# Split GELU-multiply on one core: stores issued from ScalarE's DMA queue, loads from SyncE's

## The chip, the cores and the metric

One core of one Trainium2 chip; the other cores are idle. The metric is the device time of one execution in microseconds.

## The reference

```python
# x: (32, 512, 2048) float32, standard normal
x1, x2 = x[..., :1024], x[..., 1024:]
out = (0.5 * x1 * (1 + erf(x1 / sqrt(2)))) * x2      # (32, 512, 1024) float32
```

The input is 134.2 MB and the output 67.1 MB. There is one GELU and one multiplication per output element, and no matmul.

## The kernel before

The rows are cut into 16 tiles. Each of the 128 partitions holds R = 8 consecutive rows of a tile, so a load is 8.4 MB (64 KB per partition) and a store is 4.2 MB (32 KB per partition). Both kinds of tile have two buffers. All transfers are issued from SyncE, so they stand in one queue in program order: load 0, load 1, store 0, load 2, store 1, load 3, and so on.

```python
    ahead = [load(0), load(1)]                     # load: nc.sync.dma_start(out=x_tile, in_=x_t[i])
    for i in range(n_tiles):
        x_tile = ahead.pop(0)
        o_tile = opool.tile([P, R, half], out.dtype, name="o_tile")
        pieces = 1 if i < n_tiles - 1 else 4       # the last tile is stored in four pieces
        step = R // pieces
        for k in range(pieces):
            for r in range(k * step, (k + 1) * step):
                nc.scalar.activation(out=x_tile[:, r, :half], in_=x_tile[:, r, :half], func=GELU)
                nc.vector.tensor_mul(out=o_tile[:, r, :], in0=x_tile[:, r, :half], in1=x_tile[:, r, half:])
            rows = slice(k * step, (k + 1) * step)
            nc.sync.dma_start(out=o_t[i][:, rows, :], in_=o_tile[:, rows, :])
        if i + 2 < n_tiles:
            ahead.append(load(i + 2))
```

## Time and profile before

| | before |
|---|---|
| time, median (4 runs) | 475.56 us |
| span of the profile | 472.7 us |
| DVE / ACT busy | 31% / 26% |
| DMA engines busy | 99% |
| tile 1's landing to tile 2's | 29.2 us |
| last load's landing to the end | 20.4 us |

The page of the kernel before: its row of DMA busy tenths in 40 equal slices, and the share of the 16 DMA engines' time that each queue took. Queue q1 is SyncE's; q14 is the runtime's instruction fetch.

```profile
DMA  8999999999999999999999999999999999999996
...
q1 hardware_dynamic: 5040, 201.33, 99.0%
q14 instruction: 2, 0.02, 0.0%
...
out_dram<-o_tile SPq DMA_DIRECT2D x15, 4096.0 KB, 28.5
out_dram<-o_tile SPq DMA_DIRECT2D x4, 1024.0 KB, 8.9
x_tile<-in_x_dram SPq DMA_DIRECT2D x16, 47.6
```

In the last three lines, the last column is the median time from issue to landing. A load lands 47.6 us after its issue, although its bytes need only 19.3 us at 434 GB/s. The rest is standing in the line, because the previous load and a store are ahead of it.

The table of windows of the kernel before. Its columns are the stretch and its length in us, busy time and instruction counts of three engines, the clock, the mean DMA busy share, and GB/s. The borders are the moments when a load had landed.

```profile
22.60:43.06 20.46, 9.17 (x8) 7.68 (x9) 0.00 (x0) 1.00 0.94 384
43.06:72.27 29.21, 9.17 (x8) 7.68 (x8) 0.00 (x0) 1.00 1.00 431
...
423.30:452.30 29.00, 9.17 (x8) 7.68 (x8) 0.00 (x0) 1.00 1.00 434
452.30:472.70 20.40, 9.17 (x8) 7.68 (x8) 0.00 (x0) 1.00 0.80 341
```

In the middle, the DMA share is 1.00 and compute takes a third of each period: the DMA engines bound the kernel. The last stretch has a lower share.

### The profile page before, as it was taken

To read this page: it belongs to the slowest core of one execution; us is meant where nothing else is said; L and a number is where in the kernel's file an instruction comes from. 1 tells how busy PE (TensorE), PEld (TensorE's weight loads), DVE (VectorE), ACT (ScalarE), POOL (GpSimd) and SP (SyncE) were. 2 spreads that over 40 slices of the span, in tenths; PEclk is the share of its full clock that TensorE was granted. 3 is DMA by queue.
4 is the path that set the end of the run, shared out by engine and by line. 5 is a ranking of instruction groups with operands and counts; after the bars stand their busy time and mean duration, and the time that the engine had idled before them with its cause. 6 is when DMAs were issued, how large, how long until landed. Compare 5 with 4: busy or idle time off the path is not lost.

```text
span 472.7 us, 394 instructions
## 1 busy us (share of the span) xinstructions
DVE 146.8 (31%) x128; ACT 124.2 (26%) x129; POOL 0.2 (0%) x4
## 2 busy tenths in 40 slices
DVE  0072507034070340704307043070420705206061
ACT  1053206042060410605106051050501506014060
POOL 0000000000000000000000000000000000000000
DMA  8999999999999999999999999999999999999996
GB/s 355 444 444 380 441 422 444 444 413 474 391 458 427 408 446 427 451 438 402 458 410 460 416 410 455 422 460 433 427 438 397 441 444 433 449 402 469 410 408 291
DMA packets 5042, 201.35 MB, mean 426 GB/s; under 512 B 560, under 2 KB 560, under 8 KB 560
## 3 DMA queue, kind: packets, MB, share of 16 engines
q1 hardware_dynamic: 5040, 201.33, 99.0%
q14 instruction: 2, 0.02, 0.0%
HBM read 134.22 MB, written 67.11 MB: 426 GB/s over the span
## 4 chain that ended last, share of the span: by engine, by line
DMA 79%; DVE 15%; ACT 2%; SPq 1%; issue 0%; DVEq 0%; ACTq 0%
DMA x_tile<-in_x_dram 79%; DVE o_tile L52 15%; ACT x_tile L49 2%; SPq L58 1%; DVEq L86 0%; SPq L37 0%; ACTq L49 0%
## 5 line engine op out<-in xcount | busy, mean ns | idle before, releaser
L52 DVE TENSOR_TENSOR o_tile<-x_tile 128x1024 f32<-128x1024 f32 x128 | 146.8, 1219 | 315.8 <-ACT x_tile L49 315.8
L49 ACT ACTIVATE x_tile<-x_tile 128x1024 f32<-128x1024 f32 x128 | 122.9, 1042 | 335.1 <-DMA x_tile<-in_x_dram 335.1
L49 ACT ACT_TABLE_LOAD x1 | 1.3, 1283 | 0.7 <-PEq L75 0.7
L75 POOL MEMSET const-bfloat16-1.0<- 128x1 bf16 x1 | 0.1, 102 | 0.0
L75 POOL MEMSET const-uint8-127<- 128x1 uint8 x1 | 0.1, 102 | 0.0
L75 POOL MEMSET const-float32-1.0<- 128x1 f32 x1 | 0.1, 99 | 0.0
L75 POOL MEMSET const-float32-0.0<- 128x1 f32 x1 | 0.1, 98 | 0.2 <-issue 0.2
## 6 DMA issues: line engine op xcount, KB each, us to landing
out_dram<-o_tile SPq DMA_DIRECT2D x15, 4096.0 KB, 28.5
out_dram<-o_tile SPq DMA_DIRECT2D x4, 1024.0 KB, 8.9
x_tile<-in_x_dram SPq DMA_DIRECT2D x16, 47.6
```

The lines of the kernel that those rows point to most:

```text
L49: nc.scalar.activation(out=x_tile[:, r, :half], in_=x_tile[:, r, :half], func=GELU)
L52: nc.vector.tensor_mul(out=o_tile[:, r, :], in0=x_tile[:, r, :half], in1=x_tile[:, r, half:],)
L58: nc.sync.dma_start(out=o_t[i][:, rows, :], in_=o_tile[:, rows, :])
L75: nc = _bacc.Bacc("TRN2", target_bir_lowering=False, num_devices=1)
```

## The change

Stores get a queue of their own, ScalarE's, so that loads no longer stand behind a store that waits for compute. The four stores of the last tile go out on SyncE, which has no loads left to issue by then, and so do not stand behind store 14.

```diff
-        pieces = 1 if i < n_tiles - 1 else 4
+        last = i == n_tiles - 1
+        pieces = 4 if last else 1
 ...
-            nc.sync.dma_start(out=o_t[i][:, rows, :], in_=o_tile[:, rows, :])
+            queue = nc.sync if last else nc.scalar
+            queue.dma_start(out=o_t[i][:, rows, :], in_=o_tile[:, rows, :])
```

## The prediction

> What bounds the kernel now. The DMA engines. The page gives queue q1 a 99.0% share of the 16 engines' span; DVE is 31% busy, ACT 26%. The table of windows gives one tile's period, 43.06 to 72.27 us, as 29.2 us at a DMA share of 1.00 and 431 GB/s; 423.3 to 452.3 us ran at 434 GB/s. All 201.33 MB at 434 GB/s need 464 us (estimate); the span is 472.7 us. The 9 us between lie at the two ends: the start of the first load, and the last stretch, 452.3 to 472.7 us, at a share of 0.80 and 341 GB/s.
>
> The chain of waits is 79% "DMA x_tile<-in_x_dram", 15% DVE. That looks like load latency (47.6 us from issue to landing, against 19.3 us of transfer at 434 GB/s), but most of it is standing in a full line: at its issue, most of the previous load and one store are ahead of it. Taking the store out of that line does not shorten the total line.
>
> What changes. Nothing is added or removed in bytes, transfers or compute. Fifteen 4 MB stores get issued from ACT; four 1 MB stores remain on SyncE. SyncE saves 15 issues of about 0.34 us; ACT pays about as much, 5 us in all. ACT waits 335 us for loads, and at a tile's end the next load is still some 19 us away, so this costs nothing. Load i+2 is issued about 0.45 us earlier, into a line with some 19 us of work in it: worth nothing.
>
> What moves is the order on the DMA engines. Now load i+1 passes wholly before store i. After, the two rings are served in turn: the Trainium skill ("DMA: Bandwidth & Descriptors", section "Issuing engines are not separate DMA queues") says that transfers of several issuers run on the same 16 engines and interleave, and that only issue time is saved. No run shows it yet. I expect the period to stay at 29.2 us, and store i done long before its buffer is wanted again, two tiles later.
>
> The tail. Now the last load lands at 452.3 us with about 4 MB of store 14 still to go, which covers the 10.2 us of the last tile's compute. After, store 14 shares with load 15, so the last load lands later, perhaps at 456 to 460 us, with less store work left to cover the compute; then 10.2 us of compute, about 2.4 us for the last 1 MB and 1 to 2 us to its landing. That gives 471.5 to 474.5 us of span, against 472.7. The unprofiled time stood 2.9 us above the profiled span; so about 476 us.
>
> Predicted: 476.0 us, 8 in 10 between 471.5 and 482. Faster by over 2%: 0.02 (that needs under 466 us, which the bytes hardly allow). Same: 0.91. Slower by over 2%: 0.07.
>
> What would show it. Right: DMA share 1.00 and 430 to 435 GB/s in the middle windows, a period of 29 to 29.4 us; about 63 MB on a second queue; stores landing in 19 to 30 us, loads still in 45 to 49 us; the last load landing at 455 to 460 us and a last stretch of about 15 instead of 20.4 us. Wrong: a middle rate off by over 1%, ACT's activations starting late behind a store, or a DMA share below 1.00 between tiles.
>
> What would make it wrong. If interleaving HBM reads and writes packet by packet slows the engines (435 down to 425 GB/s is 10 us), it gets slower by 2%; if the rings' alternation hides a fixed cost between transfers, up to 5 us are won. If the store ring starves load 15, the tail is uncovered by up to 10 us.

## More of the kernel before

A profile records one execution, and its span is 1.7 to 2.1 us shorter than the time of that same execution. The profiled execution of the kernel before took 474.72 us, the shortest on record for it, so its profile shows the kernel slightly better than its median.

ScalarE's timeline of the kernel before (start, length, engine, work, and in brackets its idle time before that and what ended it):

```profile
72.27 7.68 ACT L49 ACTIVATE x_tile<-x_tile 128x1024 f32<-128x1024 f32 x8 [21.53 <-DMA x_tile<-in_x_dram]
101.35 7.68 ACT L49 ACTIVATE x_tile<-x_tile 128x1024 f32<-128x1024 f32 x8 [21.40 <-DMA x_tile<-in_x_dram]
130.71 7.68 ACT L49 ACTIVATE x_tile<-x_tile 128x1024 f32<-128x1024 f32 x8 [21.68 <-DMA x_tile<-in_x_dram]
159.94 7.68 ACT L49 ACTIVATE x_tile<-x_tile 128x1024 f32<-128x1024 f32 x8 [21.55 <-DMA x_tile<-in_x_dram]
189.33 7.68 ACT L49 ACTIVATE x_tile<-x_tile 128x1024 f32<-128x1024 f32 x8 [21.71 <-DMA x_tile<-in_x_dram]
```

Each line starts when a load has landed (a tile's "period" below is the distance between two of them). The distances are 29.08, 29.36, 29.23 and 29.39 us: uneven, although every tile moves the same bytes.

## The result

| | before | after |
|---|---|---|
| time, median of 4 | 475.56 us (474.96 to 475.77) | 472.05 us (471.93 to 472.21) |
| ratio | | 0.9928, interval 0.9911 to 0.9946 |
| span | 472.7 us | 470.3 us |

The change is within 2%, and a small gain clear of the noise. The times after also scatter less: in the same rounds they lie within 0.28 us, those before within 0.81 us. Over all my comparisons the kernel before ranged from 474.75 to 476.96 us.

The page after, the same lines. Queue q10 is ScalarE's.

```profile
DMA  8999999999999999999999999999999999999998
...
q1 hardware_dynamic: 2880, 138.41, 68.4%
q10 hardware_dynamic: 2160, 62.92, 31.0%
q14 instruction: 2, 0.02, 0.0%
...
out_dram<-o_tile ACTq DMA_DIRECT2D x15, 4096.0 KB, 39.4
out_dram<-o_tile SPq DMA_DIRECT2D x4, 1024.0 KB, 5.6
x_tile<-in_x_dram SPq DMA_DIRECT2D x16, 47.6
```

Loads take the same 47.6 us to land, so the intent (loads that do not stand behind stores) is not where the gain is. Stores take 39.4 us instead of 28.5 us. That is longer than a period, so there is always a store in the line.

The table of windows after:

```profile
22.60:47.15 24.55, 9.17 (x8) 7.68 (x8) 0.00 (x0) 1.00 0.96 396
47.15:76.21 29.06, 9.17 (x8) 7.68 (x8) 0.00 (x0) 1.00 1.00 433
76.21:105.21 29.00, 9.17 (x8) 7.68 (x8) 0.00 (x0) 1.00 1.00 434
...
453.23:470.30 17.07, 9.17 (x8) 7.68 (x8) 0.00 (x0) 1.00 0.87 361
```

ScalarE's timeline after:

```profile
76.21 7.68 ACT L52 ACTIVATE x_tile<-x_tile 128x1024 f32<-128x1024 f32 x8 [21.38 <-DMA x_tile<-in_x_dram]
...
105.21 7.68 ACT L52 ACTIVATE x_tile<-x_tile 128x1024 f32<-128x1024 f32 x8 [21.31 <-DMA x_tile<-in_x_dram]
...
134.20 7.68 ACT L52 ACTIVATE x_tile<-x_tile 128x1024 f32<-128x1024 f32 x8 [21.31 <-DMA x_tile<-in_x_dram]
...
163.21 7.68 ACT L52 ACTIVATE x_tile<-x_tile 128x1024 f32<-128x1024 f32 x8 [21.33 <-DMA x_tile<-in_x_dram]
```

Now the distances are 29.00, 28.99 and 29.01 us. From tile 2's landing to tile 15's, 13 periods take 377.0 us (76.21 to 453.23) against 380.1 us before (72.27 to 452.34). So the time was in the middle of the run, where the DMA share reads 1.00 in both kernels. The two ends nearly cancel: tile 2's load lands 3.9 us later, since store work moves forward, and the last stretch is 3.3 us shorter.

### What the DMA records show

The trace holds a record of each packet of each transfer. A load gives each of the 16 DMA engines eight packets of 64 KB, and each engine ends its part of a transfer with a 4-byte record. Two readings are taken from these records throughout, and their clock is used for differences alone. The records don't name the engine; where single engines are meant, each one's packets were followed from the end of one to the start of the next.

- **Stretched packets**: load packets that took over 15 ns longer than the median (2418 ns for 64 KB), their excess summed and divided by 16, after the first 60 us.
- **Spread**: the time between the first and the last of the 16 end records of one transfer. The Trainium skill ("DMA: Bandwidth & Descriptors", section "Why a DMA increments its semaphore by 16 and not by 1") says that a transfer has landed only when every engine it uses has counted; so a load is as late as its slowest engine.

```
spread, us, at load:         1     2     5     8     11    15    last store
before                      0.67  0.73  1.39  2.17  2.91  3.48   3.36
after                       2.15  2.15  2.15  2.15  2.15  2.15   0.71

stretched load packets after 60 us:  before 88 of them, 1.06 us per engine
                                     after   2 of them, 0.05 us per engine
```

Before, the engines drift apart tile by tile. The stretched packets are the last ones of a load on each engine, the ones right before a store (85 of the 88), and some engines collect more of them than others. After, the engines differ by 2.15 us at each load's end from the first stores on, but this stays constant and the spread at the end is only 0.71 us: it is the order in which an engine takes load and store packets, not lost time.

This adds up. All transfer packets of an engine took 468.15 us on average before and 467.54 us after, 0.6 us less. The slowest engine ended 2.20 us behind the average engine before and 0.35 us after, 1.85 us less. Together that is 2.45 us, and the spans differ by 2.4 us. The medians differ by 3.5 us; the rest is not accounted for, since one execution of each kernel was profiled, and that of the kernel before was its shortest. What remained was why the packets stretch, and what the change does about it.

### The profile page after: what moved, and what is told of

It reads as the page before. It is cut to its first block, busy times and chain, and to the rows that moved or that the text cites. A ratio compares the mean times of both kernels' runs of the same rounds, so it can differ in the third digit from the quotient of the medians.

```text
span 470.3 us, 408 instructions
## 1 busy us (share of the span) xinstructions
DVE 146.7 (31%) x128; ACT 124.2 (26%) x129; POOL 0.2 (0%) x4
## 4 chain that ended last, share of the span: by engine, by line
DMA 81%; DVE 15%; ACT 2%; DVEq 0%; issue 0%; SPq 0%; ACTq 0%
DMA x_tile<-in_x_dram 81%; DVE o_tile L55 15%; ACT x_tile L52 2%; DVEq L90 0%; SPq L40 0%; ACTq L52 0%
## 6 DMA issues: line engine op xcount, KB each, us to landing
out_dram<-o_tile ACTq DMA_DIRECT2D x15, 4096.0 KB, 39.4
x_tile<-in_x_dram SPq DMA_DIRECT2D x16, 47.6
```

## The experiments

The first theory was the *boundary theory*: time is lost wherever a store follows a load in one queue. Its rivals: the gain is at the tail; it comes from loads that are issued ahead of stores; any second queue helps. The later rival is the *in-step theory*: time is lost where all 16 engines go from loads alone to stores at about the same moment, and less so once they have drifted apart. The expectations of the last four runs set it against a *queue theory*: the loss needs a store behind a load in the same queue.

| run | time, us | ratio to before | stretched load packets, us per engine | last engine behind average at the end, us |
|---|---|---|---|---|
| before (profile above) | 475.56 | 1 | 1.06 | 2.20 |
| after | 472.05 | 0.9928 | 0.05 | 0.35 |
| e1_tail_only | 480.14 | 1.0089 | 1.31 | 0.09 |
| e2_all_stores_act | 472.20 | 0.9922 | 0.05 | 0.10 |
| e3_parity | 476.18 | 1.0000 | 1.71 | 0.10 |
| e4_load_first | 475.63 | 0.9992 | 1.36 | 2.36 |
| r4_one | 475.32 | 0.9991 | 0.42 | 2.10 |
| r4_two | 473.43 | 0.9948 | 0.06 | 0.94 |
| r2_one | 477.77 | 1.0042 | 0.36 | 1.97 |
| r2_two | 476.28 | 1.0009 | 0.12 | 0.09 |
| e5_halves_two | 473.04 | 0.9974 | 0.15 (0.47 with the stores' packets) | 0.10 |
| e6_halves_one | 474.96 | 0.9979 | 0.62 (loads' and stores' packets) | 2.13 |
| e7_staggered | 482.19 | 1.0130 | 0.00 | 3.42 |
| e8_even_extra | 481.20 | 1.0113 | 1.32 | 2.61 |

In e5 and e6 the packets of loads and stores have one size, 32 KB. In e5 the queue tells them apart; in e6 it doesn't.

A small number in the last column can also mean that the last pieces waited for compute, so that the slow engines caught up (e1, e2, e3, r2_two, e5).

### e1_tail_only: the tail alone

```diff
-            queue = nc.sync if last else nc.scalar
+            queue = nc.scalar if i == n_tiles - 2 else nc.sync
```
(from the changed kernel)

> Only store 14, the last whole one, moves to ScalarE's queue; all else stays on SyncE. Boundary theory (the gain is lost time at each place where a store follows a load in one queue, unevenly over the 16 engines, so that their finishing times drift apart tile by tile): 13 of the 14 such places between tiles remain, so 474.8 to 475.8 us, ratio 0.998 to 1.001, and the spread of the engines' finish of load 15 stays near 3 us. Tail theory (the gain is that the last four stores no longer stand in line behind store 14): 472 to 473 us, ratio about 0.993.

It took 480.14 us, slower than either theory said. The tail theory falls. My number for the boundary theory missed too, for the tail's own reason. The windows of this run:

```profile
402.00:431.00 29.00, 9.12 (x9) 7.63 (x9) 0.00 (x0) 1.00 1.00 434
431.00:461.64 30.64, 3.37 (x3) 0.79 (x2) 0.00 (x0) 1.00 0.91 391
461.64:477.40 15.76, 9.17 (x8) 7.68 (x8) 0.00 (x0) 1.00 0.64 266
```

Store 14, alone in its queue, shares the engines with load 15 from its start and ends at nearly the same time: by the DMA records its last engine is done 2.7 us after the load's last. So the load lands at 461.64 instead of 452.34 us, and little is left to transfer while the last tile is computed (share 0.64). This is the uncovered tail that the prediction feared. The change does not have it, because there each store is still partly in line when the next is issued. The drift stayed (stretched packets 1.31 us per engine), as the boundary theory said.

### e2_all_stores_act: the last four stores on ScalarE as well

```diff
-            queue = nc.sync if last else nc.scalar
+            queue = nc.scalar
```

> As the changed kernel, but the last tile's four stores go out on ScalarE too. Boundary theory: the drift is gone all the same, so 471.5 to 474 us; the upper end is if waiting for VectorE on ScalarE's in-order queue delays the last rows by more than the roughly 7 us of store work still in line then. Tail theory: the four stores are again in line behind store 14, so 475 us or more.

472.20 us, as the change (472.05). The special path for the last tile is worth nothing measurable here.

### e3_parity: two queues, each with loads and stores

```diff
-        nc.sync.dma_start(out=x_tile, in_=x_t[i])
+        (nc.scalar if i >= 2 and i % 2 else nc.sync).dma_start(out=x_tile, in_=x_t[i])
 ...
-            nc.sync.dma_start(out=o_t[i][:, rows, :], in_=o_tile[:, rows, :])
+            queue = nc.scalar if i % 2 and i < n_tiles - 1 else nc.sync
+            queue.dma_start(out=o_t[i][:, rows, :], in_=o_tile[:, rows, :])
```

> Two queues, but each carries loads and stores alternately: from tile 2 on, load and store of an even tile are on SyncE, of an odd tile on ScalarE. Boundary theory in its strict form (a store right behind a load in the same queue costs, whatever the other queue does): still about 14 such places, so 474.5 to 476 us, ratio 0.998 to 1.001, spread of finishing times about 3 us. Rival (any second queue covers the loss, since an engine takes a packet of the other one in between): 471.5 to 473 us, ratio about 0.993.

476.18 us, no gain, and more stretched packets than before (1.71 us per engine). A second queue as such does nothing. The time alone would be weak evidence, since this kernel's tail is uncovered as well; the stretched packets are the evidence.

### e4_load_first: one queue, loads issued ahead of stores

```diff
+            if k == 0 and i + 2 < n_tiles:
+                ahead.append(load(i + 2))
             rows = slice(k * step, (k + 1) * step)
             nc.sync.dma_start(out=o_t[i][:, rows, :], in_=o_tile[:, rows, :])
-        if i + 2 < n_tiles:
-            ahead.append(load(i + 2))
```

> One queue (SyncE) as before, but load i+2 is issued just ahead of store i instead of just behind it. The number of places where a store follows a load is about the same. Boundary theory: 474.5 to 476.5 us, ratio 0.998 to 1.002, drift of some 3 us remains. Issue theory (loads gain by not standing behind a store): 472 to 473 us, ratio about 0.993. VectorE will wait for stores of its output buffer, and the last tile gets 20 us or more after its load; the store work still in line (12 MB, 29 us) should cover that.

475.63 us. Loads landed 39.6 us after their issue instead of 47.6 us, and it bought nothing. The issue theory falls.

### r4_one, r4_two, r2_one, r2_two: more and smaller transfers

```diff
-    R = 8
+    R = 4                      # 2 in the r2 kernels
+    depth = 16 // R            # number of buffers and of loads ahead, instead of 2
```
(r4_two and r2_two: the same edit in the changed kernel; the r2 kernels store the last tile in two pieces)

> One queue as before, but tiles of 4 rows per partition instead of 8 (4 MB loads, 2 MB stores, 32 tiles) and four buffers instead of two, so the same bytes are in flight; about twice as many places where a store follows a load (some 28 instead of 14). Boundary theory: the loss doubles if it is per place, so 2 to 4 us longer than the 8-row kernel at the same tail; the spread of the engines' finishing times reaches 5 to 7 us instead of 3.5, and the gap to its two-queue twin is 5 to 8 us. If the loss goes with the bytes and not with the places, the gap stays at 3 to 4 us.

> The 4-row kernel with the stores on ScalarE's queue, the last tile's on SyncE. Boundary theory: no drift after the first stores, 470 to 472.5 us, as the 8-row two-queue kernel or a little under it since the tail is shorter.

> One queue, tiles of 2 rows (2 MB loads, 1 MB stores, 64 tiles), eight buffers; about four times the places of the 8-row kernel. Boundary theory, per place: spread 10 us or more, gap to its two-queue twin 9 to 16 us. If the loss goes with the bytes: gap 3 to 4 us.

> The 2-row kernel with the stores on ScalarE's queue. Boundary theory: 469 to 473 us, no drift; the issue and landing of 64 smaller transfers each way stays hidden behind eight buffers.

All four expectations of a loss per place failed. With twice as many places, the gap between one queue and two was 1.9 us, and with four times as many, 1.5 us, instead of 5 us and more. A loss that goes with the bytes, a gap of 3 to 4 us, failed as well. The spread in one queue does not grow with each store; it stops:

```
spread, us, end records in order:   10th  16th  22nd  34th  58th transfer
r4_one                              2.81  3.42  3.42  3.42  3.42
```

Once the engines are some 3 us apart (3.4 us in r4_one, 2.5 to 2.9 us in most of r2_one), hardly anything more is lost. The boundary theory as a cost per place is wrong; something about the engines being in step seemed to matter. This made the in-step theory.

One of these runs already speaks against it in its plain form. In r4_two each engine takes a load packet and a store packet in turn, and the engines do so together: between 60 and 440 us, the records show 209 moments at which at least 14 of the 16 engines go from loads to stores within 0.3 us. Only 3 load packets were stretched, 0.06 us per engine. So switching over in step is not enough for the loss. In the kernel before, the switch comes after eight load packets in a row on every engine, and with the store in the same queue; which of the two matters, these runs don't separate.

These runs also price the packet size. A 64 KB packet took 2418 ns, 32 KB 1213 ns, 16 KB 611 ns, 8 KB 309 ns: two half packets take 7 to 9 ns more than a whole one. Per engine, all packets took 467.54 us in the changed kernel and 469.19 us in r4_two, 1.65 us more, enough for its 1.4 us longer time. In r2_two they took 473.86 us.

### e5_halves_two and e6_halves_one: stores that begin anew in every tile

```diff
-        nc.sync.dma_start(out=x_tile, in_=x_t[i])
+        for h in (slice(0, R // 2), slice(R // 2, R)):
+            nc.sync.dma_start(out=x_tile[:, h, :], in_=x_t[i][:, h, :])
```
(e5 from the changed kernel, e6 from the kernel before)

> Two queues as in the change, but each load goes out as two of 4 rows (32 KB packets, as large as the stores'), so a store should get half of the engines' time instead of a third, be done some 20 us after its issue, and leave about 9 us of loads alone in each tile: stores then begin anew on all engines once per tile, though no store ever follows a load in one queue. In-step theory (time is lost where all engines go from loads alone to stores together, until they have drifted apart; queues matter only in that the change keeps a store always in line): stretched load packets come back in every tile, 0.4 us per engine or more after the first 60 us, and 473.5 to 477 us. Queue theory (the loss needs a store behind a load in the same queue): under 0.1 us per engine after the first 60 us, 471.5 to 474 us.

> The one-queue twin of e5_halves_two: loads in two halves, everything on SyncE. Both theories: stretched packets in each tile and a drift of about 3 us, as before; the 32 KB packets add about 1 us (two of 1213 ns for one of 2418 ns); 475 to 477.5 us.

e5 did what it was built for. Its stores landed in 23.5 us, and the records show loads and stores at some 217 GB/s each while both run, then some 10 us of loads alone. What came back is less clear. Of the load packets, 14 were stretched, in 9 of the tiles, 0.15 us per engine: the in-step theory said 0.4 or more in every tile, the queue theory under 0.1, and neither is met. Another 41 stretched packets, 0.33 us per engine, belong to stores, most of them late in a store, where the engines go back to loads alone; the changed kernel has no such store packet. So some loss returned though no store follows a load in a queue, but mostly not at the place that the in-step theory names. The time, 473.04 us, is in the range of the queue theory (471.5 to 474 us) and just under that of the in-step theory (473.5 to 477 us); two of its six runs took 476.8 and 478.2 us. e6 took 474.96 us, just under its range, with 0.62 us of stretched packets. Part of e5's lead over e6 is the last stretch, which waits for compute and lets slow engines catch up.

### e7_staggered and e8_even_extra: one queue, engines put out of step

```diff
     ahead = [load(0), load(1)]
+    o_first = [opool.tile([P, R, half], out.dtype, name="o_tile") for _ in range(2)]
+    for j, p in enumerate((2, 5, 7, 10, 12, 15)):          # e8: (16, 16, 16)
+        row, col = 32 * (j // 2), 4 * (j % 2)
+        nc.sync.dma_start(out=o_first[1][row : row + p, col : col + 4, :].rearrange("p a b -> p (a b)"),
+                          in_=x_t[0][0:p, 0:2, :].rearrange("p a b -> p (a b)"))
```
(`o_first` are the output tiles 0 and 1; the extra data are overwritten before use, and the results were correct)

> One queue as before, but between load 1 and store 0 six small extra loads of 2, 5, 7, 10, 12 and 15 partitions (16 KB each per partition; what they bring is overwritten) go to that many engines, so the engines are put out of step by up to 3.7 us (6 packets of about 0.61 us) before the first store. In-step theory: hardly anything is lost afterwards: stretched packets after the first 60 us under 0.5 us per engine (1.2 before), the spread stays at what the extra loads made, 3.5 to 4.5 us; time about 475 to 476.5 us although 1.9 us of transfers per engine were added. Queue theory without the step: a further 2 to 3 us of drift on top, spread 5 to 6.5 us, 477 to 479 us.

> The control of e7_staggered: three extra loads of 16 partitions, the same for all 16 engines, 1.8 us per engine. Both theories: the drift and the stretched packets are as before (spread about 3.5 us at the end, 1.2 us per engine after the first 60 us), so the time is that of before plus the 1.8 us: 477 to 478 us. In-step theory: 1 to 2 us slower than e7_staggered though no more bytes are moved; queue theory: no slower than it.

The times say little, since both missed: I expected e7 to be faster than e8, and it was 1 us slower (482.19 against 481.20 us). The extra packets took about 2.1 to 2.4 us instead of 0.61 us, so the stagger became 8 us instead of 3.7 us and VectorE had to wait for it at the start. Where they went: the Trainium skill ("SBUF — State Buffer", section "Door 1: The DMA port swizzle") gives partitions 0 to 15 four of the 16 ports and about 109 GB/s, which I had not applied when I expected 0.61 us per packet. In e8, 16 packets of 16 KB into 16 partitions took 2.4 us, which is 109 GB/s.

What the loss does afterwards is clear. In e7 not one load packet was stretched after the first 60 us, and the spread at load 15 was 8.7 us against 8.2 us at load 2. In e8, with about as many extra bytes but the engines nearly in step (1.6 us apart at load 2), there were 100, 1.32 us per engine, and the spread grew to 4.47 us. The windows from tile 2's landing to tile 15's, e7 and then e8:

```profile
82.68:460.18 377.50, 119.22 (x104) 99.87 (x104) 0.00 (x0) 1.00 1.00 434
```

```profile
78.70:459.30 380.60, 119.22 (x104) 99.87 (x105) 0.00 (x0) 1.00 1.00 432
```

The same 13 periods took 377.0 us after the change and 380.1 us before. So e7 won 3.1 us on e8 in the middle, and lost 4.0 us to it before tile 2 landed; that is why it was the slower of the two. ScalarE's timeline of e7, one queue:

```profile
315.20 7.68 ACT L56 ACTIVATE x_tile<-x_tile 128x1024 f32<-128x1024 f32 x8 [21.30 <-DMA x_tile<-in_x_dram]
344.21 7.68 ACT L56 ACTIVATE x_tile<-x_tile 128x1024 f32<-128x1024 f32 x8 [21.33 <-DMA x_tile<-in_x_dram]
373.19 7.68 ACT L56 ACTIVATE x_tile<-x_tile 128x1024 f32<-128x1024 f32 x8 [21.30 <-DMA x_tile<-in_x_dram]
402.19 7.68 ACT L56 ACTIVATE x_tile<-x_tile 128x1024 f32<-128x1024 f32 x8 [21.32 <-DMA x_tile<-in_x_dram]
```

And the same view of e8:

```profile
313.28 7.68 ACT L56 ACTIVATE x_tile<-x_tile 128x1024 f32<-128x1024 f32 x8 [21.68 <-DMA x_tile<-in_x_dram]
342.35 7.68 ACT L56 ACTIVATE x_tile<-x_tile 128x1024 f32<-128x1024 f32 x8 [21.39 <-DMA x_tile<-in_x_dram]
371.96 7.68 ACT L56 ACTIVATE x_tile<-x_tile 128x1024 f32<-128x1024 f32 x8 [21.92 <-DMA x_tile<-in_x_dram]
401.03 7.68 ACT L56 ACTIVATE x_tile<-x_tile 128x1024 f32<-128x1024 f32 x8 [21.39 <-DMA x_tile<-in_x_dram]
```

Out of step, the periods shown are 29.01, 28.98 and 29.00 us with a single queue, as after the change. One of e7's 13 periods took 29.58 us (198.65 to 228.23 us), with some store packets stretched and no load packet. In step they are 29.07, 29.61 and 29.07 us.

So in one queue it is shown that the loss in the middle needs engines that are nearly in step when they go from a load to a store. Why the change removes the loss is not shown in full. Its engines mix loads and stores nearly all the time: after the first 60 us, the longest stretch without a store packet on any engine is 2.6 us, against 16 to 19 us in every tile before. But r4_two shows that engines can switch over together without loss, and e5 met neither theory. Two readings stay open: the loss may need a run of several load packets before the switch, or a store behind a load in the same queue, in both cases with the engines in step. As a cure, e7 is useless, since its stagger has to be paid: at the start, and at the end, where the slowest engine finishes 3.42 us behind the average.

## Why the prediction was right, and where it was not

The measured 472.05 us lies in the predicted range, 471.5 to 482 us, but close to its lower end and 4 us from the predicted 476.0 us. The sum behind it missed: it gave a span of 471.5 to 474.5 us, and the span was 470.3 us. It then added 2.9 us, the distance from the profile to the median of other executions, where the profiled execution itself stands 2.0 us above its span. The range held because it was wide; the bound that it rests on was right.

- *What bounds the kernel*: right. The time moved 0.7% with the DMA engines as busy as before. All experiments lie between 472 and 482 us.
- *SyncE's and ScalarE's issue time costs nothing, and the earlier issue of loads is worth nothing*: right. Loads land in 47.6 us as before, and e4, with 39.6 us, gained nothing.
- *The engines serve the two queues in turn*: right. The Trainium skill ("DMA: Bandwidth & Descriptors", section "Queues, rings and completion order") says that an engine goes round the queues that have work, a packet at a time. The runs agree: in the changed kernel, between 200 and 394 us, 960 records on q1 and 969 on q10 carried 56.0 and 28.1 MB, two to one as 64 KB and 32 KB packets are. In e5, with equal packets, the rates were about equal.
- *"The 9 us between lie at the two ends"*: wrong in part. 3.1 us were in the middle, in 13 periods of 29.24 us on average that can take 29.00 us. They were invisible in the share, since a stretched packet counts as busy.
- *"I expect the period to stay at 29.2 us"*: this is the term that was mis-sized. It became 29.00 us, and with it the time is near the lower end of the range. The prediction listed "the rings' alternation hides a fixed cost" as a way to win up to 5 us; the size fits, but the runs don't show it to be the cause: in e3 two queues that each carry loads and stores gained nothing, and e7, with one queue, needed 377.5 us for the 13 periods against 377.0 us after the change.
- *The tail*: the mechanism was right, the sizes not. Stores landed in 39.4 us, not 19 to 30, since a store gets a third of the engines and so needs about a whole period, and it starts behind the rest of the one before. The last load therefore landed at 453.23 us, not 455 to 460, and the last stretch was 17.1 us, not 15, well covered by store work. e1 shows the tail that was feared, at a cost of 4 us.

Left open: what it is in an engine, in SBUF or in HBM that stretches the last load packets before a store, why some engines are hit more often, and which trait of the change removes this (see e5, e7 and r4_two). A run that would help keeps one queue and engines in step, but has fewer load packets in a row before each store. About 1.7 us per engine are lost at the very start in both kernels (the first load packets and the first store), and no run tried to remove that. None of the versions I tried beats the change.

## What to carry to other kernels

A DMA share of 1.00 does not mean that the engines run at full speed: compare the distances of equal tiles, and the slowest engine with the average one, before calling a transfer-bound stretch perfect. Moving stores to a second queue does not add bandwidth; here it gained 0.7%, with each queue carrying one kind of transfer and a store always in line. A second queue with loads and stores in both gained nothing (e3). Where little store work is left behind the last load, the same move can cost more than it gains (e1).

## What the Trainium skill lacked or had wrong

- "DMA: Bandwidth & Descriptors", section "Issuing engines are not separate DMA queues", says that issuing from several engines only saves issue time. Here it saved 3.5 us of 475.6 us (ratio 0.9928), and not through issue time: e4 issued loads earlier and gained nothing.
- No page that I read has the loss at the last packets of a load before a store in one queue: 1.06 us per engine over 14 loads, and engines that drift 3.5 us apart; none in e7, where they start 8 us apart.
- "DMA: Bandwidth & Descriptors", section "Queues, rings and completion order", counts a packet in descriptors (9 to 17 typical) and gives no bytes there. On these queues the turn is one record of the trace, of 64 or 32 KB (how many descriptors that is, the trace doesn't tell), so bandwidth is shared in proportion to what a partition holds in one transfer: 2 to 1 in the change, about 1 to 1 in e5.
